# Sample queries times states: plain float32 products on 32-column strips in place of full-width split ones

## The chip, the cores and the metric

The kernel runs on one core of a Trainium2 chip. The metric is the device time of one execution in microseconds (us); the median of the runs shown is quoted. One profiled execution of the kernel before is read beside it.

## The reference, cut to what matters

One layer of a hybrid decoder is computed: an mLSTM branch and a gated linear attention (GLA) branch, four heads each, merged by learned gates and followed by a gated convolutional feed-forward block. There are two groups of tokens with the same weights: a prompt of 256 tokens, and 8 sample batches of 8 tokens each. Everything is float32. The sample batches bring recurrent states along, and each sample's queries have to be multiplied with the state of its own batch. These are the two products that the change touches:

```python
# mLSTM, state C [B, H, 256, 256]
num = (jnp.einsum('bhls,bshe->blhe', s, vc)
       + jnp.swapaxes(w_inter, 1, 2)[..., None] * jnp.einsum('blhd,bhde->blhe', qc, C))
# GLA, state S [B, H, 128, 256]
o = (jnp.einsum('bhts,bshe->bthe', a_mat, vc)
     + jnp.einsum('bthd,bhde->bthe', qc * jnp.exp(b), S))
```

For one head that is, for each of 8 batches, 8 query rows times a state of 256 x 256 (mLSTM) or 128 x 256 (GLA).

## The kernel before, in words

All activations are kept transposed, features on the 128 partitions and the 320 tokens (256 of the prompt, 64 of the samples) along the free axis. Every weight matrix streams from memory once through a ring of tiles (`weights`, L63): a block of 128 x 1024 lands as float32 (`raw`), ScalarE rounds it to the first float32r part (`wh`, L69) and VectorE subtracts to get the second (`wl`, L70). A product of float32 accuracy is then three float32r matmuls (`mm3`, L73): high times high, high times low, low times high (L74 to L76), each with a 128 x 128 weight block loaded into TensorE and 320 token columns streamed past it, into a PSUM tile named `big`.

The stages are: start (transposing x, the GLA query and key projections of the first two heads), the mixers (L232 to L757, a loop over four heads, each with one `gla_head` and one `mlstm_head`), the output gates, the merge, the output projection, and the feed-forward block. A scheduler in the framework orders each engine's instructions when the program is built (`schedule_with_timeline_sim`, L952); each engine then runs its own list in that fixed order and waits on semaphores. In the mixers TensorE's list holds the projections of the coming heads and of the output gates, between which the small matmuls of a head are placed.

The helper `inter` (L495) computes the sample queries times the states. It is called once by each `gla_head` (L595, `nd` = 1: the state has 128 rows) and once by each `mlstm_head` (L689, `nd` = 2: 256 rows), so eight times in all. It works as follows. The queries are spread into a tile `qz`, one 128-column block for each batch and each `d`: the high part of the batch's 8 queries in columns 8b to 8b+7, the low part in columns 64+8b to 64+8b+7, zeros elsewhere (zeroed once, L273; L501 writes the high parts, L502 the low parts). The states are split pair by pair of 128 x 256 blocks into `ch` (ScalarE, L509) and `cl` (VectorE, L510), two buffers of each. TensorE multiplies each `qz` block with `ch` and with `cl` (L514), all accumulated in one PSUM tile `mxi` whose rows 0 to 63 and 64 to 127 are later to be added. ScalarE copies it out as `si` (L518). In `numerators` (L464) one more matmul per 128 features (L479) multiplies `si` with `id2`, two identities stacked (L269, L270), which adds the halves and transposes at once.

The states are loaded by SP (L541 for GLA, L645 for mLSTM) into three buffers named `state`, and updated later by VectorE (L635, L736). Other lines that the text speaks of: L576 and L579 belong to the decay tree of a GLA head (matmul, then a predicated copy into `AT`), L655 is the load of rows that an mLSTM head broadcasts to all partitions (`bc`), first read by VectorE at L666, and L692 to L694 are the matmuls of queries and keys of an mLSTM head, which take plain float32 operands already: L692 streams 256 columns past 128 weight columns, L693 64 columns past 64, L694 128 columns past 128.

Of the kernel before, what the change touches and what calls it, by code (L numbers as in the profile page):

```python
"""Hybrid mLSTM / GLA decoder step: all activations transposed [feature, token],
weights stationary, float32 products as three float32r passes of exact splits."""
# [8 lines left out]
F32 = mybir.dt.float32  # L11
# [32 lines left out]
def step_kernel(ctx: ExitStack, tc: tile.TileContext, a: dict):  # L44
# [18 lines left out]
    def weights(src, kc, mc):  # L63
        """rows of a [kc * 128, mc * 128] block (kc * mc = 8) as two float32r tiles [128, kc, mc * 128]"""
        raw = ring.tile([P, kc, mc * P], F32, tag="raw", name="raw", bufs=RAW)
        nc.sync.dma_start(raw, src.rearrange("(k p) c -> p k c", p=P))
        hi = ring.tile([P, kc, mc * P], F32R, tag="wh", name="wh", bufs=3)
        lo = ring.tile([P, kc, mc * P], F32R, tag="wl", name="wl", bufs=3)
        nc.scalar.activation(hi, raw, AF.Copy)  # L69
        nc.vector.tensor_tensor(lo, raw, hi.bitcast(F32), op=ALU.subtract)  # L70
        return hi, lo
# [6 lines left out]
    def part_product(out, w, c0, k0, nk, xh, xl, parts=None):  # L78
        """adds the rows k0 * 128.. (four tiles) of [256 columns c0.. of w]^T @ x to two [128, N] PSUM tiles"""
        hi, lo = parts or weights(w[k0 * P:(k0 + 4) * P, c0:c0 + 256], 4, 2)  # L80
        for m in range(2):
            for kk in range(4):
                k = k0 + kk
                mm3(out[m][:, :N], hi[:, kk, m * P:(m + 1) * P], lo[:, kk, m * P:(m + 1) * P],
                    xh[k], xl[k], k == 0, k == nk - 1)

    def product(w, c0, rows, xh, xl):
        """[256 columns c0.. of w (rows, .)]^T @ x, as two [128, N] PSUM tiles."""
        out = [big(), big()]
        for k0 in range(0, rows // P, 4):  # L90
            part_product(out, w, c0, k0, rows // P, xh, xl)
        return out

# [11 lines left out]
    # loads the activation table and warms the tensor engine's clock while the first rows arrive  # L105
# [126 lines left out]
    # ================= mixers =================  # L232
    with tc.tile_pool(name="mc", bufs=1, reuse_waits="tile") as mc, \
# [24 lines left out]
        # batch (of the four of a group) that a row of a quadrant belongs to  # L258
# [9 lines left out]
        # two identities stacked: adds the two halves of the rows while transposing  # L268
        id2 = mc.tile([P, 64], F32, name="id2")  # L269
        nc.gpsimd.tensor_tensor(id2, ident[:, 0:64], ident[:, 64:128], op=ALU.add)  # L270
        # sample queries, one [128, 128] block per batch: H in columns 8b.., L in columns 64 + 8b.., zero elsewhere
        qz = mc.tile([P, 2, B * P + 64], F32R, name="qz")
        nc.gpsimd.memset(qz.bitcast(F32), 0.0)  # L273
        qzv = qz.rearrange("p d (b x) -> p d b x", x=P + S)
        # level masks of the GLA decay tree: s in the first, t in the second half of a block of 2h
# [60 lines left out]
        # log sigmoid(x) = min(x, 0) - ln(1 + exp(-|x|)), for the four GLA heads and the forget gates at once  # L336
# [4 lines left out]
        # cumulated log decays of the GLA heads  # L341
# [62 lines left out]
        # normaliser states, one column per segment and head  # L404
# [17 lines left out]
        # the sample tokens of k and v fill 128 rows per group of four batches: each quadrant of 32 rows holds  # L422
        # all of the group's tokens; H, L, H, L of k against H, H, L, L of v gives the whole product
# [4 lines left out]
        def tok4(t):  # L428
            """[128, 64] sample columns as [128, 2, 4, 32], the same for each quadrant"""
            return t.rearrange("p (g x) -> p g x", g=2).unsqueeze(2).broadcast_to([P, 2, 4, 32])  # L430

        def natural(src):
            """prompt columns of [128, 2, N] transposed -> PSUM [128 tokens, (2, 256)]"""
            pa = mx("mx7")
            for j in range(2):
                for m in range(2):
                    nc.tensor.transpose(pa[:, j * 256 + m * P:j * 256 + (m + 1) * P], src[:, m, j * P:(j + 1) * P], ident)
            return pa

        def values(v):  # L440
            """v [128, 2, N] -> natural rows, and the quadrant rows of the samples"""
# [22 lines left out]
        def numerators(name, A, vn, si):  # L464
            """per 128 features: natural values times A [128, (T x T in causal blocks, samples)], plus si"""
# [5 lines left out]
            for m in range(2):  # L471
                po = mx(name)
                ms = slice(m * P, (m + 1) * P)
                for j, oc, ac in ((0, 0, 0), (1, P, T)):
                    for v, w in ((vH, AH), (vH, AL), (vL, AH)):
                        nc.tensor.matmul(po[:, oc:T], v[:, j, ms], w[:, ac:ac + T - oc],
                                         start=(j == 0 and v is vH and w is AH), stop=False)
                nc.tensor.matmul(po[:, T:N], vt[:, ms], A[0:64, 384:448], start=False, stop=False)
                nc.tensor.matmul(po[:, T:N], si[:, ms], id2, start=False, stop=True)  # L479
                yield po[:, :N]  # L480

        def outer(out, kn, vn, w):
            """adds up prompt rows: out [128, w] = sum over tokens of kn (two parts [128, 2, 128]) x vn"""
            for j in range(2):
                for i, (k_, v_) in enumerate(((kn[0], vn[0]), (kn[0], vn[1]), (kn[1], vn[0]))):
                    nc.tensor.matmul(out, k_[:, j], v_[:, j, 0:w], start=(i == 0 and j == 0), stop=(i == 2 and j == 1))
# [8 lines left out]
        def inter(qs, states):  # L495
            """sum over the state's rows of sample queries qs [128, nd, 64] with states[b] [128, nd * 256],
            -> [128, 256], rows 0..63 and 64..127 to be added"""
            nd = qs.shape[1]
            qsv = qs.rearrange("p d (b t) -> p d b t", t=S)
            for d in range(nd):  # L500
                nc.vector.tensor_copy(qzv[:, d, :, 0:S], qsv[:, d])  # L501
                nc.vector.tensor_tensor(qzv[:, d, :, 64:64 + S], qsv[:, d], qzv[:, d, :, 0:S].bitcast(F32),  # L502
                                        op=ALU.subtract)
            pi = mx("mxi")
            for b0 in range(0, B, 2 // nd):
                src = states(b0)
                ch = wk.tile([P, 512], F32R, tag="ch", name="ch")
                cl = wk.tile([P, 512], F32R, tag="cl", name="cl")
                nc.scalar.activation(ch, src, AF.Copy)  # L509
                nc.vector.tensor_tensor(cl, src, ch.bitcast(F32), op=ALU.subtract)  # L510
                for i in range(2):
                    bb, d = (b0, i) if nd == 2 else (b0 + i, 0)
                    for part in (ch, cl):
                        nc.tensor.matmul(pi[:, 0:256], qz[:, d, bb * P:(bb + 1) * P], part[:, i * 256:(i + 1) * 256],  # L514
                                         start=(b0 == 0 and i == 0 and part is ch),
                                         stop=(bb == B - 1 and d == nd - 1 and part is cl))
# [4 lines left out]
        def head_norm(o2, wcols, i0):  # L521
            """o2: two [128, N] tiles (SBUF or PSUM) of one head -> normalised into hn[i0], hn[i0 + 1]"""
# [15 lines left out]
        def gla_head(h, q, k, v):  # L538
            """q, k: [128, N] (q scaled), v: [128, 2, N]"""
# [55 lines left out]
            si = inter(qe, lambda b0: st0[:, b0:b0 + 2].rearrange("p b e -> p (b e)"))  # L595
            o2 = list(numerators("mx13", AT, vn, si))
            head_norm(o2, ghw[:, 2 * h:2 * h + 2], 8 + 2 * h)
            # state update
# [41 lines left out]
        def mlstm_head(h, q, k, v):  # L640
# [48 lines left out]
            si = inter(qi, lambda b0: c0t[b0 // 4][:, b0 % 4].rearrange("p c e -> p (c e)"))  # L689
# [24 lines left out]
            # state update  # L714
# [44 lines left out]
    # ================= output gates of the two branches =================  # L759
# [28 lines left out]
    # ================= gated merge of the branches =================  # L788
# [23 lines left out]
    # ================= output projection, residual, second norm =================  # L812
# [25 lines left out]
    # ================= gated ConvFFN =================  # L838
# [23 lines left out]
    for p0 in range(0, NF, 8):  # L862
# [34 lines left out]
        if p0 + pn == NF:  # L897
            # last rows of the up projection, kept for the next step
# [82 lines left out]
```

## Time and profile before

| | |
|---|---|
| median of 3 runs | 1953.29 us (1950.29 to 1955.08) |
| profiled execution, span | 1950.9 us |
| TensorE matmuls busy | 1930.5 us, 99% of the span |
| TensorE weight loads busy | 1908.9 us, 98% |
| VectorE busy | 1107.0 us, 57% |
| ScalarE busy | 811.4 us, 42% |
| GpSimd busy | 332.6 us, 17% |

The span runs from the first to the last instruction of the profiled execution; the median of the runs is 2.4 us above it. "Busy" of TensorE counts from a matmul's start to its modelled end, and neighbouring matmuls overlap, so that a busy TensorE only says that it had something in flight; how fast it goes is read from the distance between starts. In the rows below PE is the matmul side of TensorE, PEld its weight loads, DVE VectorE, ACT ScalarE, POOL GpSimd, SP the engine that issues most loads.

### The profile page before, as it was taken

The numbers are of one execution on the slowest core, as the hardware profiler recorded it, in microseconds if no ns is written. First come the engines' busy times: TensorE is split into PE (matmuls) and PEld (weight loads), VectorE is DVE, ScalarE is ACT, GpSimd is POOL, SyncE is SP. The second block draws the span as 40 slices with busy tenths as digits, with TensorE's granted clock in tenths as the row PEclk, the third lists the DMA queues.
The fourth block names the chain that finished last, engine by engine and source line by source line (L and its number), as shares of the span: only waits on it lengthen the run. The fifth ranks groups of instructions, "written<-read, shape, count | busy, mean of one in ns | idle before, by whom it ended". The sixth has DMA issues, their size and how long they took to land.

```text
span 1950.9 us, 32725 instructions
## 1 busy us (share of the span) xinstructions
PE 1930.5 (99%) x13190; PEld 1908.9 (98%) x13190; DVE 1107.0 (57%) x1658; ACT 811.4 (42%) x1096; POOL 332.6 (17%) x618
## 2 busy tenths in 40 slices
PE   9999999999999999999999999999999999999997
PEld 8999999999999999999999999999999999999997
DVE  5767787878644444445655545554554555455455
ACT  5445444556533333333343324333432443343245
POOL 4221413143100000002211101110210120011014
PEclk9999999999999999999999999999999999999998
DMA  7745656575655555556444444444444444444442
GB/s 235 196 130 172 200 167 205 164 218 150 200 156 149 147 150 151 151 152 205 149 146 154 147 149 151 152 152 151 143 151 151 151 152 151 151 148 150 148 151 95
DMA packets 300224, 311.63 MB, mean 160 GB/s; under 512 B 15264, under 2 KB 292026, under 8 KB 300073
## 3 DMA queue, kind: packets, MB, share of 16 engines
q1 hardware_dynamic: 287849, 283.53, 48.0%
q0 software_dynamic: 7328, 24.50, 3.7%
q8 instruction: 103, 1.69, 0.4%
q10 hardware_dynamic: 4896, 1.52, 0.3%
q14 instruction: 48, 0.39, 0.1%
HBM read 287.03 MB, written 22.48 MB: 159 GB/s over the span
## 4 chain that ended last, share of the span: by engine, by line


## 5 line engine op out<-in xcount | busy, mean ns | idle before, releaser
L70 DVE TENSOR_TENSOR wl<-raw,wh 128x1024 fp32r<-128x1024 f32 x504 | 628.1, 1246 | 623.3 <-ACT wh L69 621.5
L69 ACT ACTIVATE wh<-raw 128x1024 fp32r<-128x1024 f32 x504 | 533.9, 1059 | 852.2 <-PE big L75 725.9
L74 PE MATMUL big<-hH,wh 128*128 128x320 f32 x2832 | 879.5, 311 | 2.5 <-ACT wh L69 2.5
L76 PE MATMUL big<-hH,wl 128*128 128x320 f32 x2832 | 879.6, 311 | 0.0
L75 PE MATMUL big<-hL,wh 128*128 128x320 f32 x2832 | 878.7, 310 | 0.0
L74 PEld LDWEIGHTS big<-hH,wh 128*128 128x128 f32 x2832 | 532.8, 188 | 3.5 <-ACT wh L69 2.6
L76 PEld LDWEIGHTS big<-hH,wl 128*128 128x128 f32 x2832 | 532.8, 188 | 1.4 <-issue 0.4
L75 PEld LDWEIGHTS big<-hL,wh 128*128 128x128 f32 x2832 | 532.8, 188 | 0.9 <-issue 0.4
L75 PE MATMUL big<-aL,wh 128*128 128x320 f32 x704 | 217.9, 310 | 0.0
L76 PE MATMUL big<-aH,wl 128*128 128x320 f32 x704 | 217.6, 309 | 0.0
L74 PE MATMUL big<-aH,wh 128*128 128x320 f32 x704 | 215.8, 309 | 0.0
L76 PEld LDWEIGHTS big<-aH,wl 128*128 128x128 f32 x704 | 132.4, 188 | 0.0
L75 PEld LDWEIGHTS big<-aL,wh 128*128 128x128 f32 x704 | 132.4, 188 | 0.0
L74 PEld LDWEIGHTS big<-aH,wh 128*128 128x128 f32 x704 | 131.8, 188 | 0.0
L876 POOL COPY conv<-u 128x2 f32<-128x2 f32 x44 | 8.2, 187 | 527.5 <-DVE u L873 527.5
L75 PE MATMUL big<-mL,wh 128*128 128x320 f32 x256 | 78.8, 309 | 0.0
L74 PE MATMUL big<-mH,wh 128*128 128x320 f32 x256 | 78.7, 309 | 0.0
L76 PE MATMUL big<-mH,wl 128*128 128x320 f32 x256 | 78.7, 309 | 0.0
L807 POOL TENSOR_TENSOR g<-g 128x320 f32<-128x320 f32 x16 | 14.6, 915 | 353.8 <-DVE g L803 353.8
L914 DVE TENSOR_TENSOR x<-big,x 128x320 f32<-128x320 f32 x96 | 46.6, 488 | 45.7 <-PE big L76 45.6
L888 POOL TENSOR_TENSOR g<-g,uc 128x256 f32<-128x256 f32 x44 | 32.6, 741 | 211.8 <-DVE g L887 211.8
L75 PE MATMUL big<-yL,wh 128*128 128x320 f32 x192 | 59.2, 308 | 0.0
(363 smaller groups left out, 1933.5 us busy)
## 6 DMA issues: line engine op xcount, KB each, us to landing
raw<-in_w_in SPq DMA_DIRECT2D x176, 512.0 KB, 3.7
raw<-in_ffn_w_up SPq DMA_DIRECT2D x88, 512.0 KB, 3.6
raw<-in_ffn_w_gate SPq DMA_DIRECT2D x88, 512.0 KB, 3.6
raw<-in_ffn_w_down SPq DMA_DIRECT2D x88, 512.0 KB, 3.5
raw<-in_w_out SPq DMA_DIRECT2D x32, 512.0 KB, 3.5
C<-in_state_mlstm_C SPq DMA_DIRECT2D x32, 256.0 KB, 6.4
o_C_s<-C POOLq DMA_DIRECT2D x32, 256.0 KB, 3.6
raw<-in_w_branch_a SPq DMA_DIRECT2D x16, 512.0 KB, 3.4
```

The source lines that it names most:

```text
L69: nc.scalar.activation(hi, raw, AF.Copy)
L70: nc.vector.tensor_tensor(lo, raw, hi.bitcast(F32), op=ALU.subtract)
L74: nc.tensor.matmul(out, wh, xh, start=first, stop=False)
L75: nc.tensor.matmul(out, wh, xl, start=False, stop=False)
L76: nc.tensor.matmul(out, wl, xh, start=False, stop=last)
L807: nc.gpsimd.tensor_tensor(sg[m], sg[m], acc[m], op=ALU.add)
L876: nc.gpsimd.tensor_copy(conv1[:, 0:2, c], u[:, T:T + 2])
L888: nc.gpsimd.tensor_tensor(g[:, 0:T], g[:, 0:T], gel[m][:, 0:T], op=ALU.mult)
L914: nc.vector.tensor_tensor(x2[k], pt[:, :N], x2[k], op=ALU.add)
```

## The change

`inter` no longer splits anything. The queries are written once, as plain float32, into a smaller `qz`: for each batch a block of 32 columns, with the batch's 8 queries in columns 0 to 7 (first group of four batches) or 8 to 15 (second group), zeros elsewhere. For each group of four batches and each `d` there are four matmuls, one for each batch, each with a 32-column weight block, reading the state tile directly and writing 32 rows of the PSUM tile of its own: batch r of the group to rows 32r to 32r+31. The two groups accumulate on the same 32 rows, their queries in different ones. The matrix that transposes the result (`sel` in place of `id2`) picks the right 16 of each 32 rows; the matmuls that use it keep their shape. The tiles `ch` and `cl`, and the instructions of L502, L509 and L510, are gone. Comments are left out of the diff.

```diff
-        id2 = mc.tile([P, 64], F32, name="id2")
-        nc.gpsimd.tensor_tensor(id2, ident[:, 0:64], ident[:, 64:128], op=ALU.add)
-        qz = mc.tile([P, 2, B * P + 64], F32R, name="qz")
-        nc.gpsimd.memset(qz.bitcast(F32), 0.0)
-        qzv = qz.rearrange("p d (b x) -> p d b x", x=P + S)
+        sel = mc.tile([P, 64], F32, name="sel")
+        nc.gpsimd.tensor_copy(sel.rearrange("p (g q t) -> p g q t", g=2, q=4),
+                              ident.rearrange("p (q g t) -> p g q t", q=4, g=4)[:, 0:2])
+        qz = mc.tile([P, 2, 272], F32, name="qz")
+        nc.gpsimd.memset(qz, 0.0)
+        qzv = qz.rearrange("p d (g x) -> p d g x", x=136)[:, :, :, 0:128].rearrange("p d g (q y) -> p d g q y", y=32)
...
-                nc.tensor.matmul(po[:, T:N], si[:, ms], id2, start=False, stop=True)
+                nc.tensor.matmul(po[:, T:N], si[:, ms], sel, start=False, stop=True)
...
-        def inter(qs, states):
+        def inter(qs, state):
             nd = qs.shape[1]
-            qsv = qs.rearrange("p d (b t) -> p d b t", t=S)
             for d in range(nd):
-                nc.vector.tensor_copy(qzv[:, d, :, 0:S], qsv[:, d])
-                nc.vector.tensor_tensor(qzv[:, d, :, 64:64 + S], qsv[:, d], qzv[:, d, :, 0:S].bitcast(F32),
-                                        op=ALU.subtract)
+                nc.vector.tensor_copy(qzv[:, d, :, :, 0:S], qs[:, d].rearrange("p (g q t) -> p g q t", g=2, q=4))
             pi = mx("mxi")
-            for b0 in range(0, B, 2 // nd):
-                src = states(b0)
-                ch = wk.tile([P, 512], F32R, tag="ch", name="ch")
-                cl = wk.tile([P, 512], F32R, tag="cl", name="cl")
-                nc.scalar.activation(ch, src, AF.Copy)
-                nc.vector.tensor_tensor(cl, src, ch.bitcast(F32), op=ALU.subtract)
-                for i in range(2):
-                    bb, d = (b0, i) if nd == 2 else (b0 + i, 0)
-                    for part in (ch, cl):
-                        nc.tensor.matmul(pi[:, 0:256], qz[:, d, bb * P:(bb + 1) * P], part[:, i * 256:(i + 1) * 256],
-                                         start=(b0 == 0 and i == 0 and part is ch),
-                                         stop=(bb == B - 1 and d == nd - 1 and part is cl))
+            for g in range(2):
+                for d in range(nd):
+                    for r in range(4):
+                        c0 = (4 * g + r) * 32
+                        nc.tensor.matmul(pi[32 * r:32 * r + 32, 0:256], qz[:, d, c0:c0 + 32], state(4 * g + r, d),
+                                         start=(g == 0 and d == 0), stop=(g == 1 and d == nd - 1))
...
-            si = inter(qe, lambda b0: st0[:, b0:b0 + 2].rearrange("p b e -> p (b e)"))
+            si = inter(qe, lambda b, d: st0[:, b])
...
-            si = inter(qi, lambda b0: c0t[b0 // 4][:, b0 % 4].rearrange("p c e -> p (c e)"))
+            si = inter(qi, lambda b, d: c0t[b // 4][:, b % 4, d])
```

## Rows read from the trace of the kernel before

**Rows 1.** Busy time by engine over the span (part 1 of the page).

```profile
PE 1930.5 (99%) x13190; PEld 1908.9 (98%) x13190; DVE 1107.0 (57%) x1658; ACT 811.4 (42%) x1096; POOL 332.6 (17%) x618
```

**Rows 2.** Windows, mixers and rest: stretch, length, busy us (instructions), clock, DMA.

```profile
50.00:500.00 450.00, 445.55 (x3089) 430.10 (x3088) 335.21 (x645) 228.02 (x356) 125.27 (x204) 1.00 0.59 176
500.00:1900.00 1400.00, 1400.00 (x9547) 1398.97 (x9547) 718.20 (x911) 527.38 (x624) 162.74 (x325) 1.00 0.50 154
```

**Rows 3.** Waits of PE, 50 to 500 us: total us, times, longest us.

```profile
PE mx L576 <- DVE AT L579: 3.0, 2, 1.9
PE mx L447 <- DVE C L736: 0.8, 2, 0.4
...
PE mx L576 <- POOL lv_z L568: 0.2, 1, 0.2
```

**Rows 4.** Groups of PE's matmuls by form, 50 to 500 us: count, busy, mean ns.

```profile
L514 PE MATMUL mxi<-ch,qz 128*128 128x256 f32 x96 | 25.5, 287 | 0.0
L514 PE MATMUL mxi<-cl,qz 128*128 128x256 f32 x96 | 24.3, 282 | 0.0
...
L692 PE MATMUL mx<-q,k 128*128 128x256 f32 x16 | 4.8, 379 | 0.0
```

**Rows 5.** Timeline of PE, matmuls of `inter` back to back: start, length (us).

```profile
162.21 0.28 PE L514 MATMUL mxi<-ch,qz 128*128 128x256 f32 x1
...
162.91 0.38 PE L692 MATMUL mx<-q,k 128*128 128x256 f32 x1
```

**Rows 6.** Timeline of PE: plain float32 matmuls, 128 and 64 weight columns.

```profile
163.13 0.38 PE L692 MATMUL mx<-q,k 128*128 128x256 f32 x1
163.44 0.27 PE L693 MATMUL mx<-q,k 128*64 128x64 f32 x1
...
163.54 0.22 PE L693 MATMUL mx<-q,k 128*64 128x64 f32 x1
163.69 0.38 PE L694 MATMUL mx<-q,k 128*128 128x128 f32 x1
...
163.91 0.28 PE L694 MATMUL mx<-q,k 128*128 128x128 f32 x1
```

**Rows 7.** Timeline, all engines: a weight load beside a running matmul.

```profile
161.97 0.28 PE L514 MATMUL mxi<-ch,qz 128*128 128x256 f32 x1
161.97 0.19 PEld L514 LDWEIGHTS mxi<-cl,qz 128*128 128x128 f32 x1
```

**Rows 8.** Window of tile `ch` alone: PE, PEld, DVE and ACT busy us (instructions).

```profile
50.00:500.00 450.00, 25.48 (x96) 18.07 (x96) 32.31 (x48) 28.35 (x48) 1.00 0.59 176
```

**Rows 9.** Instructions on tile `qz`: count, min/median/max ns, first and last start.

```profile
L501 DVE CAST qz<-qi x8: 184/192/197, 109.3 to 436.4; 128x64 fp32r<-128x64 f32 x8
...
L273 POOL MEMSET qz<- x1: 1907/1907/1907, 50.4 to 50.4; 128x2176 f32 x1
```

**Rows 10.** State loads on SP, their landing times, and the head's first product.

```profile
209.07 3.29 SPq L645 DMA_DIRECT2D C<-in_state_mlstm_C  x4
...
214.36 2.27 SPq L645 DMA_DIRECT2D C<-in_state_mlstm_C  x4
...
DMA to landing us min/median/max: 5.4/6.4/8.3
...
263.82 0.28 PE L514 MATMUL mxi<-ch,qz 128*128 128x256 f32 x1
```

**Rows 11.** One wait of VectorE with the cause, and the clock windows behind it.

```profile
108.09 0.29 DVE L666 TENSOR_TENSOR qi<-q,bc 128x128 f32<-128x128 f32 x1 [3.45 <-DMA bc<-rows]
...
110.00:112.00 2.00, 2.00 (x9) 2.00 (x8) 2.00 (x5) 0.00 (x0) 2.00 (x2) 0.50 0.01 4
112.00:114.00 2.00, 2.00 (x12) 2.00 (x12) 0.95 (x4) 1.41 (x2) 1.16 (x3) 0.70 0.79 224
```

**Rows 12.** Timeline of PE: a matmul of `inter` placed between two projections.

```profile
224.84 0.28 PE L514 MATMUL mxi<-ch,qz 128*128 128x256 f32 x1
224.96 0.31 PE L75 MATMUL big<-hL,wh 128*128 128x320 f32 x1
```

## The prediction

> **What bounds the kernel now.** I read the busy times first. TensorE has something in flight for 99% of the span, VectorE for 57%, ScalarE for 42% [rows 1]. Such a share is no pace, so the next view is the windows: all eight calls of `inter` lie between 118 and 494 us, inside the stretch of 50 to 500 us, and there TensorE is busy for 445.6 of 450 us; behind it, from 500 to 1900 us, for every one of 1400 us [rows 2]. The reader should see that all the idle time that faster helpers could give back is 450 - 445.6 = 4.5 us. The third view, TensorE's waits, says who owns it: 3.0 us are two waits for the predicated copy L579 and 0.8 us two waits for the state update L736, both on VectorE; no entry names `ch`, `cl` or `qz` [rows 3]. So the end of the kernel is set by how long TensorE's own list takes, and the change is worth what it does to that list; work taken from other engines counts only through those 4.5 us.
>
> **Removed from TensorE.** L514 stands there 96 + 96 = 192 times [rows 4]. Six starts lie between 162.21 and 162.91 us [rows 5], which is 0.70 / 6 = 0.117 us each, with the last step into the next line's matmul, so no gap hides there. 192 x 0.117 = 22.5 us. The record's own length (0.28 us) is not the price, since records overlap.
>
> **Added to TensorE.** There are 8 products in a GLA call and 16 in an mLSTM call, 24 for each head number, 96 in all. A plain float32 product is recorded as two matmuls, each with a weight load: L692 is called 8 times and has 16 records [rows 4]. I call one such record a pass. Two passes of 256 columns start 163.13 - 162.91 = 0.22 us apart [rows 5, 6]; finer, the record is 379 ns long where that of L514 is about 284 for the same columns [rows 4], so a pass holds TensorE 0.117 + 0.095 = 0.21 us. I take 0.215.
>
> No row shows two matmuls on different columns of the array, so the price of 192 passes is bounded from both sides. One after another they take 192 x 0.215 = 41.3 us. Four side by side, they take a quarter, 10.3 us. I choose between the ends by the order of the list. Matmul records start in the order of the list wherever the trace has them. In that order the two passes of one product stand next to each other and use the same strip. The second can't start before the first has streamed, and nothing behind it may pass. The first pass of the next strip then starts beside the second pass of this one. So TensorE is held for one pass, not two, per product: 96 x 0.215 = 20.6 us, and one trailing pass for each of the 8 calls, 1.7 us: 22.4 us. Two strips work side by side, never four. I take this value; it is an estimate from the rows of full-width passes.
>
> **Changing the width.** The 64-column matmul L693 stands between 128-column ones, and is the nearest row to a 32-column strip. The pass before it starts at 163.13 and L693 at 163.44: 0.31 us, less 0.215 of streaming, is 0.09 us of emptying. L693's two passes are 0.10 us apart, where 64 columns need 0.215 / 4 = 0.05: its weight load is exposed by 0.05. From its second pass to L694 it is 0.15, less 0.05: 0.10 of emptying. L694's two passes are 0.22 us apart where 128 columns need 0.11: 0.11 of exposed load [rows 6]. In and out again thus cost 0.35 us. Nothing in a call now waits between its products (the splits that paced them are gone), so I take one stretch for each call: 8 x 0.35 = 2.8 us. If the scheduler cuts the calls up by sets of four, as it now places single matmuls of `inter` between projections [rows 12], there are 24 stretches: 16 x (0.35 + 0.215) = 9.0 us more.
>
> **What the helpers lose.** ScalarE drops 48 copies, 28.4 us, and VectorE 48 subtractions, 32.3 us [rows 8], and 12 small subtractions of the size of L501. All of it lies beside TensorE's stream and is costed at nothing but the waits. The two waits for L579 end a chain whose VectorE sat 3.45 us waiting for the rows `bc` at 108 us, not for a split [rows 11]; I keep them. The two waits for L736 are for queued VectorE work; I let them go: 0.8 us. The lower bound is all 4.5 us, and the clock's dip behind the first wait: it was granted 0.50 from 110 to 112 us and 0.70 to 114 [rows 11], that is 2.0 + 1.2 us at 1.2 GHz in place of 2.4, worth half, 1.6 us.
>
> **What costs nothing.** L501 keeps its 12 copies, to a float32 `qz` of as many elements [rows 9]. The zeroing on POOL shrinks from 2176 to 544 columns (1.9 us before), and `sel` replaces `id2` one for one; TensorE waits only 0.2 us for POOL in a decay step [rows 3]. TensorE now reads states itself: a late state would stop everything queued behind it, projections included. But the loads are issued at 209 and 214 us and land in at most 8.3, and the head's first product is at 263.8 us [rows 10]. The new direct wait, for the copy into `qz`, stands ahead of the projections in the same way; were VectorE late there, its price would be a wait like those of rows 3.
>
> **The sum.** -22.5 + 22.4 + 2.8 - 0.8 = +1.9 us: span 1950.9 to 1952.8. The median stood 2.4 us above that span; I carry it over: 1955.2 us.
>
> **Rivals.** (A) The forecast: two strips overlap, 1955.2. Its own range runs from all waits and the dip gone (-4.5 - 1.6 in place of -0.8: 1949.9) to 24 stretches (1964.2). For it: the order of starts in every row of the timeline.
>
> (B) Four strips overlap, because the second pass of a product doesn't hold up the other strips: 10.3 in place of 22.4, 1943.1. Against it: passes would have to start out of their order. The Trainium skill (TensorE: Matmul & The Clock Gate, Part 3: Packing small matmuls) says that matmuls on different tiles run at once but start and end strictly in order, and gives 2.38 times for three column tiles of single-pass products. By the order this is A; by the speed-up, as an estimate, 41.3 / 2.38 = 17.4 us, between A and B. No run here shows it so far.
>
> (C) The strips don't overlap: a pass waits for the pass before it, whichever strip it is on. 41.3 in place of 22.4: 1974.1. It decides from the first call on, and it is also what comes out if the change doesn't do what it says. For it: no row shows two matmuls sharing the array. Against it: weight loads already run beside matmuls, the load for `cl` starting at the moment (161.97) at which the matmul with `ch` starts [rows 7]. The same page and part speaks for C: loads pass running matmuls only when the row groups differ, which these strips, all 128 rows high, don't. The trace disagrees at full width: the load of rows 7 has the same rows.
>
> (D) C, and each change of strip empties the array as a change of width does: 88 x (0.09 + 0.05) = 12.3 us more: 1986.4. The Trainium skill (TensorEngine Tiling, Key Properties) lets only a change of mode drain, not one of tile; no row tells.
>
> **How the numbers follow.** About 0.3% (5.9 us) is what a measurement of this kernel can tell from no change, so faster ends at 1947.4 and slower begins at 1959.2. A 0.50: of it 0.04 faster, 0.39 the same, 0.07 slower (a cut-up list). B 0.22: 0.21 faster, 0.01 the same. C 0.20 and D 0.08, both slower. Together faster 0.25, same 0.40, slower 0.35. A alone would range from 1950 to 1964. Leaving out D and the edges of B and C, the range is 1941 to 1976. Its ends are B with the idle time given back and C with two us of new waits.
>
> **What would show it.** In the profile after, the product line of `inter` should have 192 records with 32 weight columns. Under A their starts alternate, a few ns and then about 0.21 us; under B eight records start within one pass; under C each is 0.21 us behind the last, under D 0.35. ScalarE's busy time should fall by 28 us and VectorE's by 35, and the stretch from 500 us on should keep its length. Wrong would be the prediction if the calls were cut up, or if the two waits of rows 3 grew under the new order of the list.

## The result and the profile after

The changed kernel takes 1939.5 us (median of 4 runs, 1937.42 to 1940.51) where the kernel before takes 1953.41: a ratio of 0.9932, with a 95% interval of 0.9918 to 0.9946. It is 0.7% faster. That is more than the 0.3% that a measurement can tell from no change, and 1.5 us below the low end of the predicted range. The profiled execution's span went from 1950.9 to 1936.1 us.

Busy time by engine, kernel after (the line that answers to [rows 1]):

```profile
PE 1920.9 (99%) x13190; PEld 1893.8 (98%) x13190; DVE 1074.4 (55%) x1598; ACT 782.6 (40%) x1045; POOL 328.0 (17%) x618
```

TensorE has as many matmuls as before, 13190, in 14.8 us less. ScalarE fell by 28.8 us and VectorE by 32.6. The same two stretches as in [rows 2]:

```profile
50.00:500.00 450.00, 447.89 (x3190) 427.47 (x3189) 317.72 (x610) 209.96 (x325) 129.62 (x213) 1.00 0.62 186
500.00:1900.00 1400.00, 1400.00 (x9545) 1399.15 (x9544) 712.18 (x899) 524.70 (x624) 163.50 (x326) 1.00 0.50 152
```

In the mixers TensorE starts 3190 matmuls in 450 us, 101 more than before, and it is idle for 2.1 us instead of 4.5. Behind them nothing has changed: 9545 matmuls in 1400 us where there were 9547, one every 0.147 us. So the gain was made before 500 us: 106 matmuls, five of them by 50 us already, ahead of the first call of `inter` (clock there 0.97 before, 1.00 after). TensorE's largest waits there, kernel after (total us, times, longest; answers to [rows 3]; L568 and L571 are the decay tree's L576 and L579):

```profile
PE mx L568 <- DVE AT L571: 1.6, 1, 1.6
PE mx L695 <- POOL ds L693: 0.4, 1, 0.4
```

Matmuls of `inter` by form (answers to L514 in [rows 4]): 192 records as before, with 32 weight columns.

```profile
L507 PE MATMUL mxi<-C,qz 128*32 128x256 f32 x128 | 7.7, 382 | 0.0
L507 PE MATMUL mxi<-S,qz 128*32 128x256 f32 x64 | 4.9, 385 | 0.0
```

A record is as long as one of the plain float32 L692 in [rows 4] (0.38 us), but the busy time per record is about a sixth of it (12.6 us for 192): the records lie on top of each other. How closely, the timeline of TensorE shows, kernel after (start, time from the first start to the last end, count): one GLA call between its neighbours, then one mLSTM call.

```profile
115.11 0.33 PE L568 MATMUL mx<-lv_z 128*128 128x64 f32 x2
115.37 1.07 PE L507 MATMUL mxi<-S,qz 128*32 128x256 f32 x16
116.37 0.42 PE L76 MATMUL big<-hH,wl 128*128 128x320 f32 x1
116.63 0.31 PE L74 MATMUL big<-hH,wh 128*128 128x320 f32 x1
...
157.18 0.31 PE L74 MATMUL big<-hH,wh 128*128 128x320 f32 x1
157.42 1.93 PE L507 MATMUL mxi<-C,qz 128*32 128x256 f32 x32
159.28 0.70 PE L684 MATMUL mx<-q,k 128*128 128x256 f32 x2
```

Sixteen passes take 1.00 us from the first start to the next line's start, 32 take 1.86. The prediction's terms are 4 x 0.215 = 0.86 and 8 x 0.215 = 1.72 if four strips overlap, and about twice that if two do. The same view, of two short windows inside the GLA call:

```profile
115.37 0.42 PE L507 MATMUL mxi<-S,qz 128*32 128x256 f32 x4
...
115.37 0.64 PE L507 MATMUL mxi<-S,qz 128*32 128x256 f32 x8
```

At 115.39 us four passes are in flight, and by 115.70 eight have started. The sixteen starts come in four groups of four, at 115.372 to .392, 115.612 to .632, 115.828 to .848 and 116.043 to .063 us: four starts within 0.02 us, then about one pass (0.216 to 0.240 us) until the next four. A record doesn't name its strip. That four starts 0.02 us apart are on four strips is read from experiment 1, where 256-column passes on the same columns never start less than 0.215 us apart. In the list, as with L692 in [rows 5, 6], the two passes of a product should stand next to each other (strip 0 first pass, strip 0 second pass, strip 1 first pass, and so on). Then a first pass of strip 1 starts 0.2 us ahead of the second pass of strip 0, which stands before it in the list. Experiment 2 shows overtaking without this assumption.

**Where the 14.8 us went.** For a ledger I took the distance from each matmul's start to the next matmul's start, from the first one to the 2801st projection (up to 557.9 us before, 543.1 after; all small matmuls of the mixers are done by then), and added the distances up by what the matmul belongs to (us; worked out from the traces):

| | before | after | change |
|---|---|---|---|
| products of `inter` (192 records) | 23.5 | 12.0 | -11.5 |
| projections (2801 records) | 431.1 | 428.2 | -2.9 |
| all else, the start included | | | -0.4 |

The first line is the work itself. The second is the same work with fewer gaps in it (a wait of TensorE counts with the matmul ahead of it). The experiments test the two apart.

### The profile page after: what moved, and what is told of

Read it like the earlier page. It is cut to its first block, busy times and chain, and to the rows that moved or that the text cites. A ratio compares the mean times of both kernels' runs of the same rounds, so it can differ in the third digit from the quotient of the medians.

```text
span 1936.1 us, 32558 instructions
## 1 busy us (share of the span) xinstructions
PE 1920.9 (99%) x13190; PEld 1893.8 (98%) x13190; DVE 1074.4 (55%) x1598; ACT 782.6 (40%) x1045; POOL 328.0 (17%) x618
## 4 chain that ended last, share of the span: by engine, by line
## 5 line engine op out<-in xcount | busy, mean ns | idle before, releaser
L70 DVE TENSOR_TENSOR wl<-raw,wh 128x1024 fp32r<-128x1024 f32 x504 | 629.1, 1248 | 627.1 <-ACT wh L69 626.6
```

## The experiments

All times are medians; ratios are against the kernel before on the same chip. Experiments 1 to 3 shared one chip (before: 1951.81 us), 4 to 6 and a second measurement of the kernel after another (1951.68), 7 and 8 and a third measurement a third (1951.91). These two of the kernel after gave 1937.33 (0.9924, 0.9912 to 0.9937) and 1937.54 (0.9926, 0.9913 to 0.9940).

> The changed kernel once more, on the same chip as the three beside it, to compare them with: 0.993 of the time before, as measured.

> The changed kernel once more, to compare the two beside it with: 0.992 to 0.993 of the time before.

### 1: plain float32, full width

The same 192 plain passes, each on all 128 columns: blocks of `qz` 128 columns wide, with zeros beside the eight queries.

```diff
-        qz = mc.tile([P, 2, 272], F32, name="qz")
+        qz = mc.tile([P, 2, 1472], F32, name="qz")
...
-                        c0 = (4 * g + r) * 32
-                        nc.tensor.matmul(pi[32 * r:32 * r + 32, 0:256], qz[:, d, c0:c0 + 32], state(4 * g + r, d),
-                                         start=(g == 0 and d == 0), stop=(g == 1 and d == nd - 1))
+                        c0 = 128 + (4 * g + r) * 168 - 32 * r - 8 * g
+                        nc.tensor.matmul(pi[:, 0:256], qz[:, d, c0:c0 + 128], state(4 * g + r, d),
+                                         start=(g == 0 and d == 0 and r == 0), stop=(g == 1 and d == nd - 1 and r == 3))
```

> The changed kernel, still plain float32 and without splits, but each batch's queries in a block of the full 128 weight columns, all products on the same columns. Theory (the gain comes from four strips working at once): 192 passes one after another, 192 x 0.215 = 41.3 us where the strips take 24 x 2 x 0.215 = 10.3 and some 3 us of width changes; 28 us slower than the changed kernel, about 1967. Rival (the gain comes from work taken off ScalarE and VectorE, which this kernel keeps off too): no slower than the changed kernel, 1940.

Measured: 1962.79 us, ratio 1.0053 (1.0038 to 1.0068). TensorE's timeline, experiment 1, the same two calls:

```profile
116.39 3.67 PE L507 MATMUL mxi<-S,qz 128*128 128x256 f32 x16
...
159.40 7.07 PE L507 MATMUL mxi<-C,qz 128*128 128x256 f32 x32
```

Without strips the products hold TensorE for 40.9 us in the ledger, 0.213 us a pass, and the change would have been a loss. So the price of a pass was right (0.215 forecast), and the gain of the change on TensorE is the overlap of the strips: 3.67 us against 1.07 for the same 16 passes. The helpers have as little to do as in the kernel after; their relief alone doesn't carry plain float32.

### 2: strip by strip

The kernel after with the loops turned round, so that all passes of a strip stand together in the list.

```diff
-            for g in range(2):
-                for d in range(nd):
-                    for r in range(4):
+            for r in range(4):
+                for g in range(2):
+                    for d in range(nd):
```

> The changed kernel with the loop over the strips outermost: all products of strip 0, then of strip 1 and so on; same products, same widths. Theory (a strip takes its next pass when it is free, and passes of other strips behind it in the list go ahead of it, over any distance): as fast as the changed kernel, 1940. Rival 1 (passes start in the order of the list; no overlap but at the three changes of strip in a call): 13 passes in each GLA call and 29 in each mLSTM call hold TensorE, 4 x 42 x 0.215 = 36.1 us in place of 10.3, 1965. Rival 2 (passes overtake, but only over a few places in the list): the GLA calls, with 4 passes for each strip, keep more of the overlap than the mLSTM calls with 8; between the two times.

Measured: 1948.60 us, 0.9983 (0.9974 to 0.9993): by order alone, most of the gain is gone; in the ledger the products cost 22.7 us in place of 12.0. TensorE's timeline, experiment 2, the two calls, and between them short windows at 0.03 us into the first and 0.11 and 0.96 us into the second (a window shows what is in flight in it):

```profile
115.67 1.09 PE L507 MATMUL mxi<-S,qz 128*32 128x256 f32 x16
...
115.67 0.44 PE L507 MATMUL mxi<-S,qz 128*32 128x256 f32 x4
...
157.74 4.59 PE L507 MATMUL mxi<-C,qz 128*32 128x256 f32 x32
...
157.74 0.40 PE L507 MATMUL mxi<-C,qz 128*32 128x256 f32 x1
...
158.41 0.62 PE L507 MATMUL mxi<-C,qz 128*32 128x256 f32 x3
```

The GLA call, with four passes for each strip, overlaps as before: four in flight at once, 1.09 us. All four passes of a strip stand together in this list, in whichever order the passes of a product are, so the strips behind the first can only have started by overtaking it. The mLSTM call, with eight for each strip, doesn't: one pass at a time at first, then two strips (the three records of the last window; records on one strip overlap, 0.38 us long and 0.216 apart), 4.59 us where the interleaved order takes 1.93. Its first four starts are at 0, 0.24, 0.456 and 0.672 us, all of strip 0, and strip 1's first pass starts at 0.893 us, together with strip 0's fifth. So passes don't overtake without bound, as the theory had it; rival 2 comes nearest. One reading fits all these starts: TensorE takes the list in order, and each strip holds up to four passes, the running one included. Strip 0's eighth pass, behind which strip 1's first stands, finds room when the fifth starts, 4 x 0.22 = 0.89 us after the first. By this reading each strip starts 0.89 us behind the one before it, and the last of 32 passes starts at 3 x 0.89 + 7 x 0.216 = 4.18 us; measured 4.22. With four passes to a strip nothing is ever held up, as in the GLA call. The depth rests on two list orders only.

### 3: two strips of 64 columns

Two batches stand side by side in place of four; `qz` is wider, with the queries spread to fit.

```diff
...
-                    for r in range(4):
-                        c0 = (4 * g + r) * 32
-                        nc.tensor.matmul(pi[32 * r:32 * r + 32, 0:256], qz[:, d, c0:c0 + 32], state(4 * g + r, d),
+                    for r in (0, 2, 1, 3):
+                        c0 = 64 + 480 * g + 104 * r - 32 * (r % 2) - 8 * g
+                        h0 = 64 * (r // 2)
+                        nc.tensor.matmul(pi[h0:h0 + 64, 0:256], qz[:, d, c0:c0 + 64], state(4 * g + r, d),
...
```

> The changed kernel with strips of 64 columns, two batches side by side in place of four, alternating in the list. Theory (the time is the passes of one strip): half as many strips, twice the time, 96 x 0.215 = 20.6 us in place of 10.3: 10 us slower than the changed kernel, about 1950. Rival (the four strips didn't really share the array, and the gain lies elsewhere): about 1940.

Measured: 1945.72 us, 0.9966 (0.9953 to 0.9979). TensorE's timeline, experiment 3:

```profile
115.08 1.95 PE L509 MATMUL mxi<-S,qz 128*64 128x256 f32 x16
...
156.97 3.67 PE L509 MATMUL mxi<-C,qz 128*64 128x256 f32 x32
```

Two strips take half of the 3.67 us of one, four take a quarter plus the ends. In the ledger: 40.9, 23.0 and 12.0 us for one, two and four. With the strips interleaved in the list, the time of the products goes down with the number of strips. This is also what the prediction's likeliest case would have been on TensorE (22.4 us). Even then the kernel comes out 6 us faster than before, though the products cost nearly the 23.5 us of before, so something besides the products gives time back.

### 4: the splits kept, unread

The kernel after, which also makes `ch` and `cl` of every pair of blocks; no matmul reads them.

```diff
...
+            for b0 in range(0, B, 2 // nd):
+                src = pair(b0)
+                ch = wk.tile([P, 512], F32R, tag="ch", name="ch")
+                cl = wk.tile([P, 512], F32R, tag="cl", name="cl")
+                nc.scalar.activation(ch, src, AF.Copy)
+                nc.vector.tensor_tensor(cl, src, ch.bitcast(F32), op=ALU.subtract)
...
```

> The changed kernel, with the 48 copies on ScalarE and 48 subtractions on VectorE that split the states put back; TensorE doesn't read what they make. Theory (only TensorE's list counts, helpers through its waits alone): 0 to 3 us slower than the changed kernel, 1939.5 to 1942.5. Rival (relief of the helpers is a third of the gain or more): 4.5 us slower or more, 1944 and above.

Measured: 1944.11 us, 0.9959 (0.9946 to 0.9971), 6.8 us above the kernel after beside it. TensorE's waits and the mixers' window, experiment 4:

```profile
PE mx L574 <- DVE AT L577: 1.7, 4, 0.9
PE mx L609 <- DVE kd L602: 1.3, 1, 1.3
```

```profile
50.00:500.00 450.00, 446.88 (x3157) 421.87 (x3156) 344.24 (x654) 234.05 (x371) 134.58 (x216) 1.00 0.59 184
```

The window of the kernel after, second measurement:

```profile
50.00:500.00 450.00, 448.76 (x3205) 428.15 (x3204) 320.47 (x610) 209.82 (x326) 129.46 (x214) 1.00 0.60 186
```

The two profiled executions are 8.1 us apart (spans of 1942.2 and 1934.1). TensorE is idle for 3.1 us instead of 1.2: 1.9 us. The products cost 14.3 instead of 12.0: 2.3 us more, with the calls cut into 14 stretches where they were 9. That leaves 3.9 us. About one of them is in the first 50 us, ahead of all calls of `inter` (eight matmuls fewer by 50 us, at a granted clock of 0.93 in place of 1.00); the rest stays open.

### 5: the kernel before without its splits

The kernel before with one constant pair of blocks in place of `ch` and `cl`; this leaves the states out of the products. TensorE's work is the same as before, its list isn't: the scheduler puts the 192 matmuls into 8 stretches where before has 48.

```diff
...
-                src = states(b0)
-                ch = wk.tile([P, 512], F32R, tag="ch", name="ch")
-                cl = wk.tile([P, 512], F32R, tag="cl", name="cl")
-                nc.scalar.activation(ch, src, AF.Copy)
-                nc.vector.tensor_tensor(cl, src, ch.bitcast(F32), op=ALU.subtract)
+                ch, cl = c2[:, 0], c2[:, 1]
...
```

> The kernel before, without the splitting of the states: its 192 float32r matmuls read one constant tile, split once, in place of the states, so that TensorE's list stays as it was and the sample states are left out of the products. Theory: TensorE's waits in the mixers (4.5 us idle) are all that can go, and those for the rows of the first mLSTM head stay: 0 to 3 us faster than before, 1950 to 1953. Rival (helpers' relief is a third of the gain or more): 4.5 us faster or more, 1949 and below.

Measured: 1947.03 us, 0.9974 (0.9964 to 0.9985): 4.7 us less than before beside it. TensorE's longest waits and the mixers' window, experiment 5:

```profile
PE mx L577 <- DVE AT L580: 1.4, 2, 1.2
...
50.00:500.00 450.00, 448.54 (x3136) 435.37 (x3135) 318.25 (x616) 206.25 (x322) 132.26 (x218) 1.00 0.59 182
```

The products cost the same, 23.3 us; the projections lose 5.6 us of gaps in the ledger (431.1 to 425.5). In the window the idle time falls from 4.45 us [rows 2] to 1.46: 3.0 us. And the half-speed clock behind the first wait [rows 11] doesn't occur in this execution: 1.6 us by the prediction's own working. That makes 4.6 of the 6.6 us between the two profiled executions (1950.9 and 1944.3); the other 2.0 stay open. It is no account of the 4.7 us between the medians: the clocks granted to single executions overlap (0.994 to 0.998 for before on this chip, 0.995 to 0.998 here), so it isn't shown that the medians differ by a stretch of half-speed clock. By the medians the relief of the helpers alone, at unchanged work on TensorE, is worth nearly five microseconds (3 to 7 by the interval).

### 7 and 8: which helper

Experiment 4 with the copies alone (7), and with the subtractions alone (8, each now a block minus itself).

```diff
...
+                ch = wk.tile([P, 512], F32R, tag="ch", name="ch")
+                nc.scalar.activation(ch, src, AF.Copy)
...
```

```diff
...
+                cl = wk.tile([P, 512], F32R, tag="cl", name="cl")
+                nc.vector.tensor_tensor(cl, src, src, op=ALU.subtract)
...
```

> The changed kernel with the 48 copies on ScalarE put back, without the 48 subtractions; nothing reads them. Theory (the helpers' share of the gain is VectorE's time, since the waits of TensorE in the mixers end with VectorE's instructions): 0 to 1.5 us slower than the changed kernel. Rival (ScalarE's time counts as much, through the splitting of the weights): 3 us slower or more.

> The changed kernel with 48 subtractions on VectorE put back (of each state from itself, the same sizes), without the 48 copies; nothing reads them. Theory (VectorE's time): 4 us slower than the changed kernel or more, most of the 6.8 us that both together cost; of it about 0.5 us for each stretch more into which the calls are cut. Rival (ScalarE, or only both together): 0 to 2 us.

Measured: copies alone 1940.08 us, 0.9941 (0.9928 to 0.9953), 2.5 us above the kernel after beside them; subtractions alone 1946.31, 0.9969 (0.9956 to 0.9981), 8.8 above. TensorE's waits and the mixers' window, experiment 8:

```profile
PE mx L572 <- DVE AT L575: 1.9, 3, 1.3
PE mx L700 <- POOL ds L698: 1.8, 2, 1.5
PE mx L572 <- POOL lv_z L564: 0.6, 2, 0.3
```

```profile
50.00:500.00 450.00, 445.67 (x3157) 421.80 (x3156) 343.98 (x652) 207.84 (x321) 139.15 (x215) 1.00 0.59 183
```

It is mostly VectorE's time that matters: with the subtractions TensorE is idle for 4.3 us, as long as before. The copies cost more than the theory's 1.5 us and less than the rival's 3, so ScalarE's time is not shown to be free.

The wait for `ds`, 1.5 us at its longest, is VectorE's in another way. L698 on POOL started when VectorE's `D` was ready, and then took 4.30 us. In the kernel after the same instruction (L693 there) takes 0.32 us at its shortest:

```profile
269.05 4.30 POOL L698 TENSOR_TENSOR ds<-ds,D 64x64 f32<-64x64 f32 x1
269.16 1.27 DVE L506 TENSOR_TENSOR cl<-S 128x512 fp32r<-128x512 f32 x2
```

```profile
L693 POOL TENSOR_TENSOR ds<-ds,D x4: 317/631/1297, 163.1 to 446.9; 64x64 f32<-64x64 f32 x4
```

In the kernel after the 0.32 us have nothing on VectorE beside them, and the 1.30 us have L70. Here two of the put-back subtractions and, among others, L70 (from 270.37 us on) lie beside it. In experiment 4, `ds` took 0.32 to 0.64 us and TensorE had no such wait.

The two experiments don't add up: with the subtractions alone the kernel is slower than with both (4: 6.8 us above), and the wait for `ds` is part of it. Each kernel is scheduled anew and gets another list, in which other projections cover other gaps. What one list happens to give or take is of the order of these 2 us, and I couldn't separate it.

### 6: every matmul at full height

There is another change of shape that costs time on TensorE: in `numerators` the one with `vt` has 64 rows between ones of 128. This kernel pads it to 128 rows with zeros.

```diff
...
-            vt = wk.tile([64, 256], F32, tag="vt", name="vt", bufs=1)
+            vt = vtz
...
-                nc.tensor.matmul(po[:, T:N], vt[:, ms], A[0:64, 384:448], start=False, stop=False)
+                nc.tensor.matmul(po[:, T:N], vt[:, ms], A[:, 384:448], start=False, stop=False)
...
+            nc.gpsimd.memset(D[64:128, 384:448], 0.0)
```

> The changed kernel, with one more place at which TensorE changed its shape taken out: the 16 products of 64 rows of sample values in the numerators get 64 more rows of zeros, so that they use all 128 rows like their neighbours. In the changed kernel their 32 passes hold TensorE 5.8 us, 0.36 each, where 128 weight columns without a change of shape take 0.11. If a change of shape is what costs there, 2.5 us faster than the changed kernel, about 1937; if not, the same, 1939.5.

Measured: 1931.84 us, 0.9895 (0.9882 to 0.9909): 5.5 us below the kernel after beside it, and faster than both kernels. TensorE's timeline around one such matmul, the kernel after (second measurement), then experiment 6:

```profile
122.59 0.28 PE L477 MATMUL mx<-AH,vL 128*128 128x128 f32 x1
122.80 0.43 PE L479 MATMUL mx<-AT,vt 64*128 64x64 f32 x2
123.16 0.43 PE L480 MATMUL mx<-sel,si 128*128 128x64 f32 x2
123.40 0.36 PE L477 MATMUL mx<-AL,vH 128*128 128x256 f32 x1
```

```profile
122.43 0.28 PE L479 MATMUL mx<-AH,vL 128*128 128x128 f32 x1
122.55 0.38 PE L481 MATMUL mx<-AT,vtz 128*128 128x64 f32 x2
122.77 0.39 PE L482 MATMUL mx<-sel,si 128*128 128x64 f32 x2
122.96 0.36 PE L479 MATMUL mx<-AL,vH 128*128 128x256 f32 x1
```

From the first to the last of these starts it is 0.81 us with 64 rows and 0.53 with 128. Sixteen times (four heads, two branches, two halves) 0.28 is 4.5 us of the 5.5; the two profiled executions are 4.8 us apart (1934.1 and 1929.3). The expectation had 2.5 us, because it took the 16 products with `vt` alone (0.36 us is for the two passes of one product): they fell from 5.8 to 3.5 us, and as much again was given back by the matmuls ahead of and behind them. A change of height costs about what a change of width does, and here the rows of zeros are free.

Not tried: the float32r parts of before on 32-column strips, which would show what the strips give without the change of type.

## Why the prediction was wrong

**The step that failed** is the choice between the ends of the added cost. "The second can't start before the first has streamed, and nothing behind it may pass" holds for one strip and not for the array: passes of other strips do pass a waiting one. So four strips work side by side and not two: 12.0 us in the ledger, 13.0 with the weight loads exposed behind, where the forecast had 22.4 + 2.8. The reason given, that records start in the order of the list, was true of every row of before, but no two neighbouring matmuls there are on different columns. A row that shows no overtaking because there was nothing to overtake on was read as a rule. The prediction did say that no row shows two matmuls on different columns, and priced the other end rightly.

**Rival B was right in kind.** On TensorE it says 10.3 + 2.8 = 13.1 us. Measured are 12.0, plus nine exposed weight loads of about 0.11 behind the stretches, 13.0. Its 1943.1 us missed the median by 3.6 us for another reason, the helpers (below). Its sign in the profile came as told: eight first and second passes within little more than one pass. The Trainium skill (TensorE: Matmul & The Clock Gate, Part 3: Packing small matmuls) says that matmuls start and end strictly in order; here passes of strip 1 start ahead of earlier ones of strip 0, by 0.2 us in the kernel after, and in experiment 2 strip 1 starts in the GLA call 0.01 us behind strip 0, whose four passes all stand before it. So the measurement decides against that sentence for column strips.

**Removed from TensorE:** predicted 22.5 us, measured 23.5. Products in a row and single ones between projections [rows 12] do cost 0.117 to 0.119 us. The other 0.9 us are in eleven products beside a small matmul of a head, 0.17 to 0.23 us each.

**Changing the width:** predicted 0.35 us for each stretch, 8 stretches. Measured in the rows above: into strips 157.42 - 157.18 = 0.24, less 0.147 for the projection, 0.09; out 0.31 from the last pass (158.976) to 159.285, less 0.215, 0.09; the load exposed behind, 116.63 - 116.37 = 0.26, less 0.147, 0.11. That is 0.29 us, in 9 stretches: one call was cut in two. Right.

**What the helpers lose** is the second term that was mis-sized: 0.8 us predicted, 4.7 measured at unchanged work (experiment 5). The lower bound, 4.5 + 1.6 = 6.1, held it. The step that went wrong was to put both waits for L579 down to the rows `bc` [rows 11]. The first one, 1.9 us, does hang on them, and it stayed: 1.6, 0.6 and 0.7 us in the three profiles of the kernel after, 1.2 in experiment 5. In one and the same program, the kernel after, it goes with the load: from its issue to its landing `bc` took 5.3, 4.1 and 4.3 us in these three profiles (4.8 before). VectorE's wait for it in the first and in the second:

```profile
104.65 0.29 DVE L658 TENSOR_TENSOR qi<-q,bc 128x128 f32<-128x128 f32 x1 [3.22 <-DMA bc<-rows]
```

```profile
104.02 0.30 DVE L658 TENSOR_TENSOR qi<-q,bc 128x128 f32<-128x128 f32 x1 [1.24 <-DMA bc<-rows]
```

The second wait for L579 is 320 us later, and no `bc` is in it. Ahead of L579 stands an instruction of the output gates that had waited for ScalarE (kernel before):

```profile
428.33 0.90 DVE L771 TENSOR_TENSOR y<-s,y 128x320 fp32r<-128x320 f32 x1 [0.80 <-ACT y L770]
...
429.42 0.66 PE L576 MATMUL mx<-lv_z 128*128 128x64 f32 x4 [1.12 <-DVE AT L579]
```

This wait is gone in the kernel after and in experiment 5, and so are the two for L736, as forecast. TensorE's idle time in the mixers, 4.5 us before, is 2.1 and 1.2 us in the first two profiles of the kernel after and 1.5 in experiment 5; it is back at 4.3 with VectorE's subtractions (experiment 8). What else is in the 4.7 us stays open.

**What costs nothing:** right. No wait for a state or for `qz` appears among TensorE's waits, and POOL's smaller zeroing shows nowhere. VectorE's relief was 32.6 us in place of 35, ScalarE's 28.8 in place of 28.

**Rivals C and D** are refuted: experiment 1 is C's price (40.9 us) on real columns, and the strips take a third of it. C's time, 1974.1, was too high even for full width, 1962.79, by the helpers' relief and the width changes that full width doesn't need, and by what lists and chips differ in.

**The sum again,** with the measured sizes: products 13.0 - 23.5 = -10.5 us, helpers -4.7, together -15.2, against -13.9 in the first comparison and -14.4 in the other two. The two come from different kernels with different lists, and the 1 us between them is within the interval of the 4.7.

**The range.** Its low end, 1941, doesn't follow from the prediction's own terms. It is named as rival B with the idle time given back, and that is 1943.1 - (4.5 - 0.8) = 1939.4 us, with the clock's dip 1937.8. Added up so, the range would have reached the measured 1939.5, by rival B and not by the forecast.

## What to carry to other kernels

Where many small products have few output rows, put them on column strips of TensorE and interleave the strips in the list: here plain float32 passes on four strips cost 12.0 us where the split full-width products cost 23.5, and the same passes 22.7 in strip-by-strip order. When no row of a profile shows a resource being shared, the order that unshared work keeps is no evidence for how shared work will be ordered; give both ends like chances. And where TensorE is the bound in a list that a scheduler makes, work taken from a helper can be worth most of TensorE's idle time in that stage (4.5 us before, 1.5 in experiment 5). Trace each wait by itself: of two waits with one name, one hung on a load and stayed, the other on a helper's queue and went.

## What the runs showed of the hardware that was not expected

Passes on different column strips overtake each other in TensorE, by what looks like four passes held for each strip; more than that in a row on one strip stops the others (4.59 us for 32 passes against 1.93).

A change of row height, from 128 to 64 rows and back, costs as a change of width does (0.29 us): 0.28 us for each of 16 places.

One instruction of GpSimd, `ds` on 64 x 64 elements, took 0.32 us with VectorE idle beside it, 1.30 beside L70, and 4.30 beside two subtractions and L70 (experiment 8).

The clock's half level follows the wait in the first GLA head, and that wait goes with the landing of `bc`, which differs between executions of one program. Windows of the kernel after (the clock is the number ahead of the last two), first and second profile:

```profile
106.00:108.00 2.00, 0.37 (x4) 0.28 (x3) 2.00 (x9) 0.75 (x2) 0.20 (x1) 1.00 0.20 20
108.00:110.00 2.00, 1.97 (x11) 1.62 (x11) 2.00 (x6) 1.14 (x2) 1.66 (x3) 0.79 0.74 242
110.00:112.00 2.00, 2.00 (x10) 2.00 (x9) 1.90 (x6) 0.43 (x2) 1.35 (x2) 0.50 0.29 39
```

```profile
106.00:108.00 2.00, 1.37 (x10) 1.01 (x9) 2.00 (x10) 1.36 (x2) 0.82 (x2) 1.00 0.41 117
108.00:110.00 2.00, 1.98 (x15) 1.72 (x15) 2.00 (x4) 0.53 (x2) 1.66 (x2) 1.00 0.42 145
110.00:112.00 2.00, 2.00 (x17) 1.87 (x15) 1.66 (x6) 1.03 (x2) 1.18 (x3) 1.00 0.59 167
```

Where TensorE stood idle for 1.6 of the 2 us, the clock was granted 0.79 in the next window and 0.50 (1.2 GHz) from 110 to 112 us, and TensorE has 10 matmuls there where the second profile has 17. Where it was idle for 0.6, the clock stayed at 1.00 (2.4 GHz). The spans are 1936.1 and 1934.1 us. Together, a wait that was 1 us longer went with a span 2 us longer.
